# Spreading the token scales of the first stage with TensorE in place of a round trip through DRAM

## The chip, the cores and the metric

The kernel runs on one core of a Trainium2 chip. The metric is the device time of one execution in microseconds (us), as the median over several runs. The core has five engines that work side by side and wait for one another by semaphores: TensorE (PE, matrix products and transposes), VectorE (DVE), ScalarE (ACT), GpSimd (POOL) and SyncE (SP). Here SP issues every DMA transfer, in the order of its own queue.

## The reference

Two layers of a mixer block, one batch of 2048 tokens and 256 context tokens, width 1024. Cut to what matters here:

```python
def rmsnorm(x, g):
    y = xf * lax.rsqrt(jnp.mean(xf * xf, axis=-1, keepdims=True) + NORM_EPS)
    return y * g
...
hx = rmsnorm(x, g_pre) * (1 + scale[:, None]) + shift[:, None]
hc = rmsnorm(ctx, g_pre) * (1 + scale_c) + shift_c
q, k, v, ga, uf, gf, zc, bc, cc, gc = split_cols(hx @ w_in, PROJ_SIZES)
...   # the same columns for hc; rotary on q and k
a = window_attention(q, k, v, kc, vc, sink_b)
f = fourier_mix(uf, w_fourier)
s = short_conv_mix(zc, bc, cc, conv_w, conv_b)
y = gated_merge(a, ga, f, gf, s, gc, w_out)
x_new = x + gate[:, None] * rmsnorm(y, g_post)
```

The step that matters is the first norm of layer 0. Every token has one scale, the rsqrt of its mean square, and the whole row of that token is multiplied by it before the product with `w_in`.

## The kernel before

Tokens are worked on in two halves of 1024 and in chunks of 512 (`CH`); the context is a chunk of 256. A product in float32 is made of three products of split operands: every operand is a high part (`hi`, `wh`) and the rest (`lo`, `wl`), and `proj_k` issues `wh` by `hi`, `wh` by `lo` and `wl` by `hi` (lines 278, 279, 280) for each of 8 blocks `k` of the width. PE contracts over partitions, so tokens must lie along the free dimension, and the width along the 128 partitions.

The first chunk of layer 0 is brought there by PE transposes (line 230, tile `pt`). The later chunks and the context of layer 0 are loaded from a second copy of the input that is transposed already, `xT` and `cT`. There the scale of a token lies along the free dimension, and every partition needs the whole row of scales. The path before is this:

- `pt_r` loads the tokens in the normal layout, one token to a partition, squares them on ACT (`jk`, line 245; `accum_out` gives the sums `ssq`), and takes the rsqrt on POOL (`ru`, `ry`, `rt`, `rr`, lines 96 to 104). The result `rr` has 128 partitions by one column for every 128 tokens. It is stored to a row `rd[slot]` in DRAM (line 248).
- `pt_load` reads the row back onto all 128 partitions (`rb` or `rbc`, line 253) and then loads the transposed input (line 255).
- `pt_post` makes for each `k` the product of input, gain `G` and row (`ht`, DVE, line 266), the high part with the shift added (`big` or `cxh`, ACT, line 267) and the low part (`big` or `cxl`, DVE, line 268).

Slot 3 is the second chunk of half 0, slot 2 the context, slots 0 and 1 the two chunks of half 1, whose scales are worked out at the end of half 0's first products.

`startup` interleaves the modulation vectors, the first chunk and its first four products (`accs`) by a string of letters, `START`; in it `r` calls `pt_r` for slot 3 and the `y`s load and advance `pt_post`. After it come, in `half`, the evacuations of chunk 0 (a SiLU gate `sg`, ACT line 754; rotary of q and k by `qk_chunk`, lines 319 to 324, which use `cosT` and `sinT`), the four products of chunk 1, of the context, and then `form_b`, ten products of 128 tokens each (`accb`, lines 376 to 378) whose outputs leave by `vt` (ACT 382, DVE 383, store to `vs` at 385) and `ut` (ACT 388, store to `us` at 389). `vt` and `ut` have two buffers, the accumulators of tag `acc` four. Then `fft_setup` loads the constants `wf` and `cf` (lines 398 and 400) and multiplies them on PE (`pa`, line 405). `form_b_w` loads and splits the weights of `form_b` (`wbh`, `wbl`). A scheduler orders the instructions of each engine when the kernel is built; at run time every engine goes through its own list in order.

Of the kernel before, what the change touches and what calls it, by code (L numbers as in the profile page):

```python
# [18 lines left out]
NCTX = 256  # L19
# [48 lines left out]
class Kern:  # L68
# [23 lines left out]
    def rsqrt(self, pool, ssq, n, tag, fast=False):  # L92
# [10 lines left out]
        r = pool.tile([128, n], F32, name=f"rr{tag}", tag=f"rr{tag}")  # L103
# [132 lines left out]
    def pt_r(self, slot, base, n, ctx, xt=None):  # L236
# [10 lines left out]
        r = self.rsqrt(self.xp, ssq[:, :nt], nt, "0")  # L247
        nc.sync.dma_start(self.rd[slot, :n].rearrange("(i p) -> p i", p=128), r)

    def pt_load(self, slot, base, n, ctx, rb, tiles):  # L250
        nc = self.nc
        m = KT // len(tiles)
        nc.sync.dma_start(rb, self.rd[slot:slot + 1, :n].broadcast_to([128, n]))
        for i, t in enumerate(tiles):
            nc.sync.dma_start(t, self.I["cT" if ctx else "xT"][:, i * m:(i + 1) * m, base:base + n])
        return [t[:, k] for t in tiles for k in range(m)], rb
# [138 lines left out]
    def fft_setup(self, l, fp, ps):  # L395
        nc = self.nc
        wf = fp.tile([128, 2, 128], F32, name="wf", tag="fbq")
        nc.sync.dma_start(wf, self.I["wf"][l].rearrange("t m d -> m t d"))
        cf = fp.tile([128, 2, 128], F32, name="cf", tag="fd")
        nc.sync.dma_start(cf, self.I["cf"])  # L400
# [218 lines left out]
    def startup(self, ps, hx, blocks, st, wps, gps):  # L619
# [65 lines left out]
        def step(c):  # L685
# [30 lines left out]
            elif c == "r" and "r" not in tail:  # L716
                tail["r"] = 1
                self.pt_r(3, CH, CH, False, self.x1)
            elif c == "y":
                if post1 is None:  # L720
                    step("r")
                    while posts < KT:
                        step("p")
                    tail["h"] = (self.big(), self.big())
                    xT = self.pt_load(3, CH, CH, False, self.x1q.tile([128, CH], F32, name="rb3"),
                                      [t.rearrange("p (k c) -> p k c", c=CH) for t in self.xts()])
                    post1 = self.pt_post(xT, tail["h"], CH, False)
                else:
                    next(post1, None)
# [10 lines left out]
    def half(self, l, half, ps, sv, tail):  # L740
# [4 lines left out]
        with ExitStack() as es:  # L745
# [49 lines left out]
            if first:  # L795
# [6 lines left out]
                with ExitStack() as e0:  # L802
                    gps = self.pool(e0, "gps", bufs=1, side="right")
                    Ws0, accs, p1, hx[1] = self.startup(ps, hx[0], blocks0, st, wps, gps)
# [12 lines left out]
            if not first:  # L817
                if half == 0:
                    hx[1] = self.hx1
                else:  # L820
                    hx[1] = (self.big(), self.big())
                    p1 = self.pt_post(self.x1, hx[1], CH, False) if l == 0 else \
                        self.p0_post(l, ps, "tr", self.x1, hx[1], CH, False)
            chunks = [(hx[c], CH, False, NCTX + base + c * CH,
                       (cosT[:, c * CH:(c + 1) * CH], sinT[:, c * CH:(c + 1) * CH])) for c in range(2)]
            wbs = ExitStack()
            if first:
                xs = [self.x1q.tile([128, D], F32, name=f"xc{i}", tag=f"xq{i}") for i in range(4)]
                self.p0_load(0, 0, NCTX, True, xs[:2])
                self.pt_r(2, 0, NCTX, True, xs)  # L830
                xc = self.pt_load(2, 0, NCTX, True, self.x1q.tile([128, NCTX], F32, name="rbc", tag="xq0"),
                                  [t.rearrange("p (k c) -> p k c", c=NCTX) for t in xs[2:]])
# [5 lines left out]
                pc = self.pt_post(xc, cx, NCTX, True)  # L838
                for k in range(KT):
                    next(p1, None)  # L840
                    for i, (j, ev) in enumerate(blocks0):
                        self.proj_k(accs[i], Ws0[i], h, n, k)
                        if i == 2:
                            next(pc)
                            if k == KT - 1:
                                self.x1pool.close()
                                wb = self.pool(wbs, f"wb{l}{half}", bufs=1)
# [9 lines left out]
            else:  # L857
# [6 lines left out]
                else:  # L864
# [5 lines left out]
                    run(gfs, mid)  # L870
                wb = self.pool(wbs, f"wb{l}{half}", bufs=1)
# [95 lines left out]
            if half == 0:  # L967
                self.x1pool = ExitStack()
                xq = self.pool(self.x1pool, f"xq{l}1", bufs=1, side="right")
                if l == 0:  # L970
                    x0 = self.pt_load(0, HALF, CH, False, st.tile([128, CH], F32, name="rb0", tag="rt", bufs=2),
# [521 lines left out]
```

## Time and profile before

| what | value |
|---|---|
| median of 3 runs | 2089.26 us (2084.22 to 2091.58) |
| span of the profiled execution | 2093.9 us; no other time of this execution is at hand |
| PE busy in it | 1980.6 us, 95% |
| mean granted PE clock | 0.983 |
| DVE, ACT, POOL busy | 59%, 41%, 36% |

The profile is of one execution. A row of a timeline has the start, the duration, the engine, line and operation, and in brackets how long the engine was idle before it and what ended that. A row of waits has the engine and line that waited, what it waited for, the sum, the number of times and the longest. The granted clock is what the chip gave to PE, as a share of full speed. Lines such as L278 are lines of the kernel before; the changed kernel has other numbers for the same code.

### The profile page before, as it was taken

To read this page: it belongs to the slowest core of one execution; us is meant where nothing else is said; L and a number is where in the kernel's file an instruction comes from. 1 tells how busy PE (TensorE), PEld (TensorE's weight loads), DVE (VectorE), ACT (ScalarE), POOL (GpSimd) and SP (SyncE) were. 2 spreads that over 40 slices of the span, in tenths; PEclk is the share of its full clock that TensorE was granted. 3 is DMA by queue.
4 is the path that set the end of the run, shared out by engine and by line. 5 is a ranking of instruction groups with operands and counts; after the bars stand their busy time and mean duration, and the time that the engine had idled before them with its cause. 6 is when DMAs were issued, how large, how long until landed. Compare 5 with 4: busy or idle time off the path is not lost.

```text
span 2093.9 us, 28506 instructions
## 1 busy us (share of the span) xinstructions
PE 1980.6 (95%) x10218; PEld 1671.9 (80%) x10218; DVE 1233.3 (59%) x2218; ACT 855.5 (41%) x1745; POOL 748.0 (36%) x967
## 2 busy tenths in 40 slices
PE   6787999999999899999999999999999989999998
PEld 2686877788788688888887888888887778888886
DVE  7343876445552677777777614333554277777775
ACT  6241211321322556666666412132222266666663
POOL 4221322231432444444444414233243254444443
PEclk9899999999999999999999999999999999999999
DMA  7678666444735744433332625124564654434421
GB/s 303 114 192 223 188 211 219 140 154 137 210 127 163 207 116 122 120 106 106 103 104 106 206 80 130 61 95 122 157 186 136 178 157 113 106 107 111 117 75 41
DMA packets 190333, 295.68 MB, mean 141 GB/s; under 512 B 17624, under 2 KB 121840, under 8 KB 189168
## 3 DMA queue, kind: packets, MB, share of 16 engines
q1 hardware_dynamic: 190192, 293.87, 47.8%
q8 instruction: 80, 1.31, 0.3%
q14 instruction: 61, 0.50, 0.1%
HBM read 218.43 MB, written 75.39 MB: 140 GB/s over the span
## 4 chain that ended last, share of the span: by engine, by line
PE 69%; DMA 10%; DVE 10%; issue 4%; POOL 3%; ACT 2%; SPq 1%; POOLq 0%; DVEq 0%; ACTq 0%
PE acc L280 8%; PE acc L279 8%; PE acc L278 8%; PE tp L1127 6%; PE yp L1176 6%; PE yp L1178 6%; PE yp L1177 6%; PE sp L1081 4%; PE op L1141 3%; PE op L1140 3%; PE sp L1078 3%; PE accb L378 2%; PE accb L376 2%; PE accb L377 2%; DVE jm L161 2%
## 5 line engine op out<-in xcount | busy, mean ns | idle before, releaser
L278 PE MATMUL acc<-big,wh 128*128 128x512 f32 x1152 | 458.9, 399 | 30.6 <-ACT big L267 11.5
L280 PE MATMUL acc<-big,wl 128*128 128x512 f32 x1152 | 454.6, 395 | 4.2 <-POOL wl L90 2.9
L279 PE MATMUL acc<-big,wh 128*128 128x512 f32 x1152 | 455.0, 395 | 0.4 <-POOL big L90 0.4
L90 POOL TENSOR_TENSOR wl<-wr,wh 128x1024 fp32r<-128x1024 f32 x63 | 158.4, 2515 | 400.5 <-ACT wh L84 272.7
L88 DVE TENSOR_TENSOR pl<-tp,ph 128x512 fp32r<-128x512 f32 x320 | 219.2, 687 | 105.6 <-ACT ph L84 102.5
L278 PEld LDWEIGHTS acc<-big,wh 128*128 128x128 f32 x1152 | 219.7, 191 | 75.2 <-ACT big L267 12.0
L1091 ACT ACTIVATE pt<-pt,nm 128x640 f32<-128x640 f32 (+2 forms) x272 | 216.2, 795 | 118.6 <-DVE nm L1088 118.2
L280 PEld LDWEIGHTS acc<-big,wl 128*128 128x128 f32 x1152 | 219.3, 190 | 51.8 <-POOL wl L90 4.0
L279 PEld LDWEIGHTS acc<-big,wh 128*128 128x128 f32 x1152 | 219.7, 191 | 43.7 <-POOL big L90 1.0
L84 ACT ACTIVATE ph<-tp 128x512 fp32r<-128x512 f32 x320 | 188.4, 591 | 132.6 <-PE tp L1127 126.2
L1102 POOL TENSOR_SCALAR pt<-pt,rv 128x640 f32<-128x640 f32 (+2 forms) x272 | 214.2, 808 | 27.2 <-DVE rv L1100 24.2
L1088 DVE CUSTOM_DVE_ANT_0 pt<-sp,mask,nsink 128x640 f32<-128x640 f32 (+2 forms) x256 | 213.4, 841 | 10.1 <-PE sp L1078 5.2
L1127 PE MATMUL tp<-ident,pt 128*128 128x128 f32 x1280 | 196.8, 274 | 12.7 <-POOL pt L1102 12.2
L1127 PEld LDWEIGHTS tp<-ident,pt 128*128 128x128 f32 x1280 | 158.6, 140 | 59.9 <-POOL pt L1102 19.2
L323 POOL TENSOR_TENSOR rs<-rs,sinT 128x512 f32<-128x512 f32 x40 | 68.1, 1703 | 183.6 <-DVE rs L321 154.1
L1081 PE MATMUL sp<-kseg,qt 128*128 128x384 f32 (+1 forms) x512 | 127.5, 330 | 1.1 <-DMA kseg<-ks 1.1
L1176 PE MATMUL yp<-big,hfh 128*128 128x512 f32 x272 | 118.1, 434 | 1.5 <-ACT big L84 1.5
L1078 PE MATMUL sp<-kctx,qt 128*128 128x256 f32 x544 | 114.2, 291 | 3.9 <-DMA qt<-qs 2.1
L1176 PE MATMUL yp<-big,hah 128*128 128x512 f32 x272 | 117.0, 431 | 0.0
L1078 PEld LDWEIGHTS sp<-kctx,qt 128*128 128x128 f32 x544 | 95.3, 189 | 18.4 <-DVE nm L1088 3.3
L1178 PE MATMUL yp<-big,hfl 128*128 128x512 f32 x272 | 107.5, 395 | 0.2
L1177 PE MATMUL yp<-big,hfh 128*128 128x512 f32 x272 | 107.1, 394 | 0.0
(373 smaller groups left out, 3711.5 us busy)
## 6 DMA issues: line engine op xcount, KB each, us to landing
wr<-in_wina SPq DMA_DIRECT2D x76, 512.0 KB, 3.8
qt<-qs SPq DMA_DIRECT2D x34, 512.0 KB, 5.0
wmt<-in_wmodt SPq DMA_DIRECT2D x32, 512.0 KB, 4.2
ftb<-ftd SPq DMA_DIRECT2D x36, 384.0 KB, 3.8
xt<-in_x SPq DMA_DIRECT2D x26, 512.0 KB, 6.4
kseg<-ks SPq DMA_DIRECT2D x24, 512.0 KB, 8.7
xt<-x SPq DMA_DIRECT2D x24, 512.0 KB, 4.5
gat<-gas SPq DMA_DIRECT2D x34, 256.0 KB, 3.2
```

The source lines that it names most:

```text
L88: self.last_v = nc.vector.tensor_tensor(lo, src, f(hi), op=ALU.subtract)
L278: nc.tensor.matmul(a, wh[:, k, :], hi[:, k, :n], start=(k == 0), stop=False)
L279: nc.tensor.matmul(a, wh[:, k, :], lo[:, k, :n], start=False, stop=False)
L280: nc.tensor.matmul(a, wl[:, k, :], hi[:, k, :n], start=False, stop=(k == KT - 1))
L1078: nc.tensor.matmul(sp[:, 256:512], B.q[:, h, :], self.kctx[:, kv, x, :], start=(x == 0), stop=(x == 1))
L1088: nc.vector.tensor_tensor_reduce(d, x, m, scale=-0.125, scalar=self.nsink[:, h:h + 1], op0=ALU.add, op1=ALU.min, accum_out=nm[:, hh:hh + 1])
L1091: nc.scalar.activation(pt, pt, AF.Exp, bias=nm[:, hh:hh + 1], scale=-1.0, accum_out=sm[:, hh:hh + 1])
L1102: nc.gpsimd.tensor_scalar(B.pts[kv][g], B.pts[kv][g], rv[:, g:g + 1], 1.0, op0=ALU.mult, op1=ALU.mult)
L1127: nc.tensor.transpose(tp[:, hh * 128:(hh + 1) * 128], pts[hh][:, t * 128:(t + 1) * 128], self.ident)
L1176: nc.tensor.matmul(yp, hh, wh[:, k, :], start=(i == 0), stop=False)
L1177: nc.tensor.matmul(yp, hh, wl[:, k, :], start=False, stop=False)
L1178: nc.tensor.matmul(yp, hl, wh[:, k, :], start=False, stop=(i == KT - 1))
```

## The change

The scales stay in SBUF (`rk[slot]`). A new `pt_row` spreads them: for each 128 tokens DVE multiplies the identity matrix by zero and adds the token's scale of its partition, which fills a 128 by 128 block `ht` with the scale of each partition along its row; PE transposes it into PSUM (`prb`), where each partition then holds the row; and ACT copies the PSUM tile to `rb`. The row in DRAM, its store and its loads are gone.

Loads are issued elsewhere. Half of chunk 1's `xT` goes to two tiles `xTa` right behind `pt_r`'s own loads, the context in its normal layout ahead of the other half, and `cT` behind that, all within `startup`; `cosT` and `sinT` thus come behind them. `wf` and `cf` are loaded into a pool of their own by `load_wcf`, ahead of `form_b`'s weights, not in `fft_setup`. The same holds for layer 1 and the second halves wherever `fft_setup` runs.

```diff
@@ -89,7 +89,7 @@
         else:
             nc.gpsimd.tensor_tensor(lo, src, f(hi), op=ALU.subtract)
 
-    def rsqrt(self, pool, ssq, n, tag, fast=False):
+    def rsqrt(self, pool, ssq, n, tag, fast=False, r=None):
         g = self.nc.gpsimd
         e = self.nc.vector if fast else g
         u = pool.tile([128, n], F32, name=f"ru{tag}", tag=f"ru{tag}")
@@ -100,7 +100,8 @@
         e.tensor_tensor(t, y, y, op=ALU.mult)
         e.tensor_tensor(t, t, u, op=ALU.mult)
         e.tensor_scalar(t, t, -0.5, 1.5, op0=ALU.mult, op1=ALU.add)
-        r = pool.tile([128, n], F32, name=f"rr{tag}", tag=f"rr{tag}")
+        if r is None:
+            r = pool.tile([128, n], F32, name=f"rr{tag}", tag=f"rr{tag}")
         e.tensor_tensor(r, y, t, op=ALU.mult)
         return r
 
@@ -244,16 +245,25 @@
             jk = self.xp.tile([128, D], BF16, name="jk", tag="jk", bufs=1)
             self.last_sq = nc.scalar.activation(jk, xt[i], AF.Square, bias=0.0, scale=1.0,
                                                 accum_out=ssq[:, i:i + 1])
-        r = self.rsqrt(self.xp, ssq[:, :nt], nt, "0")
-        nc.sync.dma_start(self.rd[slot, :n].rearrange("(i p) -> p i", p=128), r)
-
-    def pt_load(self, slot, base, n, ctx, rb, tiles):
-        nc = self.nc
-        m = KT // len(tiles)
-        nc.sync.dma_start(rb, self.rd[slot:slot + 1, :n].broadcast_to([128, n]))
+        self.rk[slot] = self.cp.tile([128, nt], F32, name=f"rk{slot}")
+        self.rsqrt(self.xp, ssq[:, :nt], nt, "0", r=self.rk[slot])
+
+    def pt_load(self, base, n, ctx, tiles, m, k0=0):
         for i, t in enumerate(tiles):
-            nc.sync.dma_start(t, self.I["cT" if ctx else "xT"][:, i * m:(i + 1) * m, base:base + n])
-        return [t[:, k] for t in tiles for k in range(m)], rb
+            k = k0 + i * m
+            self.nc.sync.dma_start(t, self.I["cT" if ctx else "xT"][:, k:k + m, base:base + n])
+        return [t[:, k] for t in tiles for k in range(m)]
+
+    def pt_row(self, slot, n, ps, rb):
+        nc = self.nc
+        w = self.xp.tile([128, CH], F32, name="ht", tag="ht", bufs=2)
+        pb = ps.tile([128, CH], F32, name="prb", tag="fft")
+        for i in range(n // 128):
+            sl = slice(i * 128, (i + 1) * 128)
+            nc.vector.tensor_scalar(w[:, sl], self.ident, 0.0, self.rk[slot][:, i:i + 1], op0=ALU.mult, op1=ALU.add)
+            nc.tensor.transpose(pb[:, sl], w[:, sl], self.ident)
+        nc.scalar.copy(rb, pb[:, :n])
+        return rb
 
     def pt_post(self, T, h, n, ctx):
         nc = self.nc
@@ -394,10 +404,7 @@
 
     def fft_setup(self, l, fp, ps):
         nc = self.nc
-        wf = fp.tile([128, 2, 128], F32, name="wf", tag="fbq")
-        nc.sync.dma_start(wf, self.I["wf"][l].rearrange("t m d -> m t d"))
-        cf = fp.tile([128, 2, 128], F32, name="cf", tag="fd")
-        nc.sync.dma_start(cf, self.I["cf"])
+        wf, cf = self.wcf
         AB = fp.tile([128, 2, 2, 2, 128], F32R, name="AB")
         pa = ps.tile([128, 2, 2, 128], F32, name="pa", tag="fft")
         for x in range(2):
@@ -716,15 +723,24 @@
             elif c == "r" and "r" not in tail:
                 tail["r"] = 1
                 self.pt_r(3, CH, CH, False, self.x1)
+                t = [gps.tile([128, D], F32, name="xTa", tag=f"wmg{i}") for i in range(2)]
+                tail["T"] = self.pt_load(CH, CH, False, [u.rearrange("p (k c) -> p k c", c=CH) for u in t], 2)
             elif c == "y":
                 if post1 is None:
                     step("r")
                     while posts < KT:
                         step("p")
                     tail["h"] = (self.big(), self.big())
-                    xT = self.pt_load(3, CH, CH, False, self.x1q.tile([128, CH], F32, name="rb3"),
-                                      [t.rearrange("p (k c) -> p k c", c=CH) for t in self.xts()])
-                    post1 = self.pt_post(xT, tail["h"], CH, False)
+                    xs = self.xs = [self.x1q.tile([128, D], F32, name=f"xc{i}", tag=f"xq{i}") for i in range(4)]
+                    self.p0_load(0, 0, NCTX, True, xs[:2])
+                    xT = tail["T"] + self.pt_load(CH, CH, False, [t.rearrange("p (k c) -> p k c", c=CH)
+                                                                  for t in self.xts(2)], 2, 4)
+                    self.xcT = self.pt_load(0, NCTX, True, [t.rearrange("p (k c) -> p k c", c=NCTX) for t in xs[2:]], 4)
+                    tail["T"] = xT
+                    post1 = iter(())
+                elif "T" in tail:
+                    rb = self.pt_row(3, CH, ps, self.x1q.tile([128, CH], F32, name="rb3"))
+                    post1 = self.pt_post((tail.pop("T"), rb), tail["h"], CH, False)
                 else:
                     next(post1, None)
 
@@ -799,9 +815,9 @@
                 xq = self.pool(self.x1pool, "xq0", bufs=1, side="right")
                 self.x1q = xq
                 self.x1 = [xq.tile([128, D], F32, name=f"xq{i}") for i in range(4)]
-                with ExitStack() as e0:
-                    gps = self.pool(e0, "gps", bufs=1, side="right")
-                    Ws0, accs, p1, hx[1] = self.startup(ps, hx[0], blocks0, st, wps, gps)
+                e0 = ExitStack()
+                gps = self.pool(e0, "gps", bufs=1, side="right")
+                Ws0, accs, p1, hx[1] = self.startup(ps, hx[0], blocks0, st, wps, gps)
             else:
                 hx[0] = self.hx0
             cosT = st.tile([128, HALF], F32, name="cosT", tag="cosT")
@@ -821,29 +837,36 @@
                     hx[1] = (self.big(), self.big())
                     p1 = self.pt_post(self.x1, hx[1], CH, False) if l == 0 else \
                         self.p0_post(l, ps, "tr", self.x1, hx[1], CH, False)
+            def load_wcf():
+                if half == 1 or not last_l:
+                    wcp = self.pool(es, f"wcf{l}{half}", bufs=1)
+                    self.wcf = [wcp.tile([128, 2, 128], F32, name=n) for n in ("wf", "cf")]
+                    nc.sync.dma_start(self.wcf[0], self.I["wf"][l].rearrange("t m d -> m t d"))
+                    nc.sync.dma_start(self.wcf[1], self.I["cf"])
+
             chunks = [(hx[c], CH, False, NCTX + base + c * CH,
                        (cosT[:, c * CH:(c + 1) * CH], sinT[:, c * CH:(c + 1) * CH])) for c in range(2)]
             wbs = ExitStack()
             if first:
-                xs = [self.x1q.tile([128, D], F32, name=f"xc{i}", tag=f"xq{i}") for i in range(4)]
-                self.p0_load(0, 0, NCTX, True, xs[:2])
-                self.pt_r(2, 0, NCTX, True, xs)
-                xc = self.pt_load(2, 0, NCTX, True, self.x1q.tile([128, NCTX], F32, name="rbc", tag="xq0"),
-                                  [t.rearrange("p (k c) -> p k c", c=NCTX) for t in xs[2:]])
+                self.pt_r(2, 0, NCTX, True, self.xs)
                 _, n, ctx, tok, rp = chunks[0]
                 for (j, ev), acc in zip(blocks0, accs):
                     ev(acc, n, ctx, tok, rp)
                 h, n, ctx, tok, rp = chunks[1]
                 accs = [ps.tile([128, CH], F32, name="acc", tag="acc") for _ in range(4)]
-                pc = self.pt_post(xc, cx, NCTX, True)
                 for k in range(KT):
                     next(p1, None)
+                    if k == 1:
+                        xc = (self.xcT, self.pt_row(2, NCTX, ps, self.x1q.tile([128, NCTX], F32, name="rbc", tag="xq0")))
+                        pc = self.pt_post(xc, cx, NCTX, True)
                     for i, (j, ev) in enumerate(blocks0):
                         self.proj_k(accs[i], Ws0[i], h, n, k)
-                        if i == 2:
+                        if i == 2 and k:
                             next(pc)
                             if k == KT - 1:
+                                e0.close()
                                 self.x1pool.close()
+                                load_wcf()
                                 wb = self.pool(wbs, f"wb{l}{half}", bufs=1)
                                 WB = self.form_b_w(l, wb)
                         if k == KT - 1:
@@ -868,6 +891,7 @@
                         self.drain(p1)
                         self.x1pool.close()
                     run(gfs, mid)
+                load_wcf()
                 wb = self.pool(wbs, f"wb{l}{half}", bufs=1)
                 fetch(J_K)
                 WB = self.form_b_w(l, wb)
@@ -968,10 +992,11 @@
                 self.x1pool = ExitStack()
                 xq = self.pool(self.x1pool, f"xq{l}1", bufs=1, side="right")
                 if l == 0:
-                    x0 = self.pt_load(0, HALF, CH, False, st.tile([128, CH], F32, name="rb0", tag="rt", bufs=2),
-                                      [t.rearrange("p (k c) -> p k c", c=CH) for t in self.xts()])
-                    self.x1 = self.pt_load(1, HALF + CH, CH, False, xq.tile([128, CH], F32, name="rb1"),
-                                           [xq.tile([128, KT // 2, CH], F32, name=f"xT{i}") for i in range(2)])
+                    x0 = (self.pt_load(HALF, CH, False, [t.rearrange("p (k c) -> p k c", c=CH) for t in self.xts()], 2),
+                          self.pt_row(0, CH, ps, st.tile([128, CH], F32, name="rb0", tag="rt", bufs=2)))
+                    self.x1 = (self.pt_load(HALF + CH, CH, False,
+                                            [xq.tile([128, KT // 2, CH], F32, name=f"xT{i}") for i in range(2)], 4),
+                               self.pt_row(1, CH, ps, xq.tile([128, CH], F32, name="rb1")))
                 else:
                     self.x1 = [xq.tile([128, D], F32, name=f"xq{i}") for i in range(4)]
                     x0 = self.xts()
@@ -1359,7 +1384,7 @@
             self.mask = self.cp.tile([128, 768], F32, name="mask")
             self.G, self.mo, self.mv = {}, {}, {}
             self.ftd = dp.tile([9, 128, 2, 384], F32, name="ftd")
-            self.rd = dp.tile([4, CH], F32, name="rd")
+            self.rk = {}
             self.ggd = dp.tile([DEPTH, 2, D], F32, name="ggd")
             x1 = dp.tile([SEQ, D], F32, name="x1")
             c1 = dp.tile([NCTX, D], F32, name="c1")
```

How it moves the instructions is shown at three places. Names: `rd` is the row in DRAM, `xq` and `xc` are tiles of chunk 1 and of the context, `gs` the stored gate. SP's list before, from the tokens of chunk 1 on:

```order
L196 DMA xq_112<-in_x 128x1024
L196 DMA xq_113<-in_x 128x1024
L809 DMA cosT<-in_cosT 128x1024
L810 DMA sinT<-in_sinT 128x1024
L815 DMA cw_91<-in_convw 128x6
L248 DMA rd<-rr_611 128x4x1
L816 DMA cbias_92<-in_convb 128x2
L196 DMA xc_712<-in_ctx 128x1024
L253 DMA rb_637<-rd 128x512
L255 DMA xt<-in_xT 128x2x512 x4
L196 DMA xc_713<-in_ctx 128x1024
L255 DMA xc_714<-in_cT 128x1024
```

and after:

```order
L254 DMA xTa<-in_xT 128x2x512 x2
L197 DMA xc_639<-in_ctx 128x1024
L197 DMA xc_640<-in_ctx 128x1024
L254 DMA xt<-in_xT 128x2x512 x2
L254 DMA xc_641<-in_cT 128x1024
L254 DMA xc_642<-in_cT 128x1024
L825 DMA cosT<-in_cosT 128x1024
L826 DMA sinT<-in_sinT 128x1024
L831 DMA cw_90<-in_convw 128x6
L832 DMA cbias_91<-in_convb 128x2
L771 DMA gs_81<-sg 128x512 x2
L844 DMA wf<-in_wf 128x2x128
```

The store and the load of the row have gone from between the tokens and `xT`; the rotary tables have moved from ahead of them to behind, and `wf`, with `cf` behind it, stands here. ACT's list before, from the last squares of chunk 1 on:

```order
L245 ACTIVATE jk,ssq<-xq_113 128x1024
L232 ACTIVATE ht<-pt,mo_153,G_154 128x512
L245 ACTIVATE jk,ssq<-xc_712 128x1024
L754 ACTIVATE sg<-acc 128x512 x2
L267 ACTIVATE big<-ht,mo_153 128x512 x2
L319 COPY rt<-acc 128x512 x2
```

and after:

```order
L246 ACTIVATE jk,ssq<-xq_112 128x1024
L233 ACTIVATE ht<-pt,mo_152,G_153 128x512
L246 ACTIVATE jk,ssq<-xc_639 128x1024
L246 ACTIVATE jk,ssq<-xc_640 128x1024
L265 COPY rb_657<-prb 128x512
L770 ACTIVATE sg<-acc 128x512
L277 ACTIVATE big<-ht,mo_152 128x512
```

Both squares of the context now stand ahead of chunk 1's work, and the copy of the row behind them. The four transposes of slot 3 (`prb` for chunk 1) stand in PE's list 15 matmuls behind the last transposes of chunk 0. Those of the context stand among the products of chunk 1; PE's list after there:

```order
L290 MATMUL acc<-big,wl 128x512
L288 MATMUL acc<-big,wh 128x512
L289 MATMUL acc<-big,wh 128x512
L264 MATMUL prb<-ident,ht 128x128
L290 MATMUL acc<-big,wl 128x512
L288 MATMUL acc<-big,wph 128x512
L289 MATMUL acc<-big,wph 128x512
L264 MATMUL prb<-ident,ht 128x128
```

where before there were matmuls alone. The two spreads that they wait for stand in DVE's list between the rotary steps of chunk 0 and the context's `pt_post`:

```order
L88 TENSOR_TENSOR ql<-rt,qh 128x512
L334 TENSOR_TENSOR rt<-rt,rs 128x512
L278 SCALAR_TENSOR_TENSOR big<-ht,mo_152,big 128x512
L263 TENSOR_SCALAR ht<-ident,rk_728 128x128
L88 TENSOR_TENSOR ql<-rt,qh 128x512
L263 TENSOR_SCALAR ht<-ident,rk_728 128x128
L276 SCALAR_TENSOR_TENSOR ht<-xc_641,G_153,rbc 128x256 x2
```

The first of the two has to let a rotary step (`ql`) pass before the second can follow; before, the context's `ht` stood there directly.

More of the change, by code (lines that the diff above doesn't have):

```diff
@@ L246, in pt_r @@
                                                 accum_out=ssq[:, i:i + 1])
-        r = self.rsqrt(self.xp, ssq[:, :nt], nt, "0")
-        nc.sync.dma_start(self.rd[slot, :n].rearrange("(i p) -> p i", p=128), r)
-    def pt_load(self, slot, base, n, ctx, rb, tiles):
-        nc = self.nc
-        m = KT // len(tiles)
-        nc.sync.dma_start(rb, self.rd[slot:slot + 1, :n].broadcast_to([128, n]))
-        for i, t in enumerate(tiles):
-            nc.sync.dma_start(t, self.I["cT" if ctx else "xT"][:, i * m:(i + 1) * m, base:base + n])
-        return [t[:, k] for t in tiles for k in range(m)], rb
+        self.rk[slot] = self.cp.tile([128, nt], F32, name=f"rk{slot}")
+        self.rsqrt(self.xp, ssq[:, :nt], nt, "0", r=self.rk[slot])
+    def pt_load(self, base, n, ctx, tiles, m, k0=0):
+        for i, t in enumerate(tiles):
+            k = k0 + i * m
+            self.nc.sync.dma_start(t, self.I["cT" if ctx else "xT"][:, k:k + m, base:base + n])
+        return [t[:, k] for t in tiles for k in range(m)]
+    def pt_row(self, slot, n, ps, rb):
+        nc = self.nc
+        w = self.xp.tile([128, CH], F32, name="ht", tag="ht", bufs=2)
[6 more added lines that the diff above has]
+        return rb
     def pt_post(self, T, h, n, ctx):
```

## The prediction

> **What bounds the kernel now.** I read the page's head first, then the waits of TensorE (PE) in the stage that the change touches, then the same stage in 5 us windows, then the chain.
>
> ```profile
> span 2093.9 us, 28506 instructions
> PE 1980.6 (95%) x10218; PEld 1671.9 (80%) x10218; DVE 1233.3 (59%) x2218; ACT 855.5 (41%) x1745; POOL 748.0 (36%) x967
> ```
>
> PE is busy 95% of the span, so 113 us are all that removing waits could give. The waits of PE from 40 to 215 us (in total, how often, the longest) say how much of it sits around the change:
>
> ```profile
> PE acc L278 <- ACT big L267: 11.5, 1, 11.5
> PE acc L278 <- ACT ut L388: 6.6, 1, 6.6
> PE acc L278 <- ACT sg L754: 5.7, 1, 5.7
> PE pa L405 <- DMA cf<-in_cf: 5.6, 1, 5.6
> PE accb L376 <- ACT ut L388: 1.1, 1, 1.1
> ```
>
> Five gaps, 30.5 us. What stands around them is seen in the windows (columns: PE, PEld, DVE, ACT, POOL busy; granted clock; DMA share; GB/s):
>
> ```profile
> 65.00:70.00 5.00, 3.69 (x16) 2.65 (x15) 0.00 (x0) 0.00 (x0) 0.00 (x0) 1.00 0.88 31
> 80.00:85.00 5.00, 4.78 (x10) 3.43 (x11) 4.87 (x9) 4.18 (x8) 1.26 (x1) 0.50 1.05 406
> 90.00:95.00 5.00, 5.00 (x24) 4.07 (x23) 5.00 (x7) 1.91 (x3) 0.96 (x1) 1.00 1.01 75
> 160.00:165.00 5.00, 5.00 (x30) 5.00 (x29) 0.29 (x1) 0.51 (x2) 2.40 (x1) 1.00 1.28 24
> 170.00:175.00 5.00, 0.47 (x1) 0.48 (x2) 0.29 (x1) 0.65 (x2) 0.00 (x0) 0.59 0.80 301
> ```
>
> Two things are to be seen. In and after the long gaps the granted clock is 0.50 to 0.59, so a gap costs more than its length. And at 65 and at 160 us the DMA engines are taken while they move 24 to 31 GB/s: something small clogs them. The chain from 54 to 200 us (start, duration) names it:
>
> ```profile
> 56.56 1.16 ACT jk L245 x2
> ...
> 58.08 1.04 POOL ry L98
> ...
> 60.27 10.15 DMA rd<-rr
> 70.86 7.72 DMA xt<-in_xT
> 78.67 0.76 DVE ht L266
> 79.45 0.73 ACT big L267
> ...
> 89.23 5.48 DMA rd<-rr
> ...
> 105.48 0.40 DVE ht L266
> ...
> 134.53 0.45 SPq L248
> 135.03 13.71 DMA xt<-in_x
> ...
> 160.31 13.05 DMA vs<-vt
> ...
> 181.98 2.71 DMA cf<-in_cf
> 184.82 2.05 PE pa L405 x8
> ```
>
> The store of the scale row (512 numbers of 4 bytes, each a piece of its own in DRAM, L248) takes 10.15 us; the row's load and those of xT stand behind it in SP's queue, so chunk 1 starts late. A third such store is issued at 134.53, and the fourth stands in SP's queue a little ahead of the vs store of 160.31; the transfers issued next to them take 13.71 and 13.05.
>
> **The change, gap by gap.** What a gap costs with its slow tail, from PE's timeline (start, duration, idle before):
>
> ```profile
> 80.22 0.79 PE L278 MATMUL acc<-big,wh 128*128 128x512 f32 x1 [11.53 <-ACT big L267]
> 85.74 0.40 PE L278 MATMUL acc<-big,wh 128*128 128x512 f32 x1
> 85.97 0.39 PE L279 MATMUL acc<-big,wh 128*128 128x512 f32 x1
> ...
> 111.00 0.58 PE L278 MATMUL acc<-cxh,wh 128*128 128x256 f32 x1 [5.72 <-ACT sg L754]
> 116.43 0.28 PE L280 MATMUL acc<-cxh,wl 128*128 128x256 f32 x1
> ...
> 174.53 0.79 PE L278 MATMUL acc<-big,wh 128*128 128x512 f32 x1 [6.58 <-ACT ut L388]
> 177.94 0.39 PE L280 MATMUL acc<-big,wl 128*128 128x512 f32 x1
> ...
> 186.52 0.77 PE L279 MATMUL acc<-big,wh 128*128 128x512 f32 x1
> 188.20 0.39 PE L280 MATMUL acc<-big,wl 128*128 128x512 f32 x1
> ```
>
> Gap 1, the row of chunk 1. From 80.22 to 85.74 stand 12 matmuls, at 0.46 where full clock gives 0.23 (85.74 to 85.97): 5.52 - 12 x 0.23 = 2.8 lost. With the 11.53 of idling 14.3. What replaces the bounce: POOL has the scales just before 60.27, as now. Four multiplications of the identity on VectorE (DVE), 128 x 128; four PE transposes; one ScalarE (ACT) copy of 128 x 512. The rows next of kin:
>
> ```profile
> 60.44 0.60 PE L230 MATMUL pt<-ident,xt 128*128 128x128 f32 x4
> 61.95 0.43 DVE L82 CAST big<-ht 128x512 fp32r<-128x512 f32 x1 [5.28 <-ACT ht L232]
> 80.75 1.05 ACT L319 COPY rt<-acc 128x512 f32<-128x512 f32 x2
> ```
>
> DVE is idle for 5.28 us before 61.95, and four products cost at most 4 x 0.40 (a 128 x 256 one at 105.48), so the spread is free and ends near 61.9. The transposes come 15 matmuls (3.5 us) after the pt transposes of 60.44, so near 64.3; they take up to 0.6 of PE. PE idles 11.53 up to 80.22, so chunk 0 ends at 68.7, and near 69.3 now. The copy stands on ACT behind the last ht (to 61.9, since the cast waits for it) and the two squares of the context, 1.16 each (64.2), needs the transposes (64.9) and takes 0.53: 65.4. Then ht 0.76, big 0.73 and lo as long as ht give 67.7: chunk 1 is ready 1.6 us ahead of PE. The first two xT loads go out ahead of the context's, which wait only for the squares of chunk 1's first tiles, done before the 56.56 ones; both are out some 3 us or more before that, near 50 and 53 (counted by hand), and have 8 us or more to land; the second two near 61.5, first used at k = 4, eleven us after the start (12 matmuls of 0.23 a k, 2.75). So gap 1 goes whole. Its cover is those 1.6 us, and the loads of the context, which must land before their squares; nothing is stored word by word then. If they land at 66, PE waits 2 to 3.
>
> Gap 2, the context. Its bounce (89.23) goes, and cT is loaded near 62, in front of all of chunk 1. From 111.00 to 116.43 stand 25 starts (two unrecorded) at 0.21; at 0.115 they would take 2.9: 2.5 lost, 8.2 with the gap. New: two spreads, which the DVE queue holds behind the rotary work of chunk 0, and two PE transposes in PE's own queue among the matmuls of k = 1 of chunk 1 and after. PE comes to the second near 81.5; DVE, which is full in the window at 90 (5.00 of 5.00), is there between 81 and 84 when its rows of before are counted from the new start. So PE waits 0 to 3; I take 2, nearer the upper end since DVE has no idle time there. Behind it stand a copy and, for eight k, ht and lo at 0.40 and an ACT step between: some 7.4 us, done near 93, when PE has chunk 1 behind it. That tie may leave 0 to 1.
>
> Gap 3, 1.1 us: an accb of form_b waits for an ACT copy that is behind squares, and these behind the 13.71 of xt. Gap 4: 6.58 plus 177.94 - 174.53 - 8 x 0.23 = 1.6, is 8.2: the last ut waits for vt, vt for the buffer that the 13.05 store holds. Both go if the word stores do, since transfers then take what their like take (KB each, median to landing):
>
> ```profile
> xt<-in_x SPq DMA_DIRECT2D x26, 512.0 KB, 6.4
> ```
>
> Bounds: nothing, if the other loads and not the words slow these; 9.3 if all goes. I take all: 24 GB/s at a full share is what words look like, and the 301 GB/s at 170 us, after them, is what the loads look like.
>
> The Trainium skill ("DMA: Bandwidth & Descriptors", Specifications) puts the least transfer for full rate at 512 B; below it the engine reads, modifies and writes. By that rule the words clog, and the window at 160 us agrees. By the same page's fixed 2 us for a transfer alone ("Anatomy of one DMA") a bounce would cost some 4 us, and an estimate from that would leave gaps 3 and 4 unexplained; the 10.15 decides against it.
>
> Gap 5, 5.55: PE waits for cf, issued at 181.98. Now wf and cf are issued behind the cT and gs rows, near 68 us, with 80 us to land. With the slow tail (188.20 - 186.52 - 4 x 0.23 = 0.8) and eight pa products at half clock (2.05, against 1.2 by the four of 60.44) it is 7.2.
>
> Moved past in SP's queue: cosT and sinT, which were loaded ahead of the scale row, go behind xT and cT now, near 64; the 3 MB from 61 on take 7 to 10 us at the 301 to 406 GB/s of the windows: landed by 72. Their first user on DVE stood here:
>
> ```profile
> 87.18 0.68 DVE L322 TENSOR_TENSOR rt<-rt,cosT 128x512 f32<-128x512 f32 x1
> ```
>
> that is 7.0 us after the start of chunk 1, near 76 then: covered by 4 us.
>
> For the second half: eight spreads in the DVE queue among ql and vt, eight transposes on PE after form_b (two times 0.6, 1.2) and two ACT copies beside PE's work. The four spreads of the last slot stand before the fourth vt and wait for that slot's last square; form_b's accb wait in gap 3 came four accumulators after the late one, so there is some 12 us of cover. Price 0 to 3, taken 0.
>
> **Sum.** 14.3 + 8.2 + 1.1 + 8.2 + 7.2 = 39.0 saved; 0.6 + 0.3 + 1.2 for transposes and 2.0 of waiting are 4.1 added: 34.9. The profiled execution spans 2093.9, 4.6 above the median of the runs (2089.3) and 2.3 above the highest. That gives 2059.0 in the profile and 2054.4 by the median; I say 2054. From 190 us on nothing that bounds PE is touched, so what is won stays.
>
> The clock after a short gap:
>
> ```profile
> 150.94 0.44 PE L376 MATMUL accb<-wbh,big 128*128 128x384 f32 x1 [1.11 <-ACT ut L388]
> ```
>
> The next matmul takes 0.44, not the 0.58 to 0.79 of the long gaps, so I price the 2 us at the context without a slow tail; with gap 1's, 2.8, they would be 4.8. The Trainium skill ("TensorE: Matmul & The Clock Gate", Part 1) halves the clock only after an idle window of about 3.4 us; by that, too, 2 us cost no more than 2.
>
> **Rivals.** (A) Part of it: the head of chunk 1 closes, later gaps stay or return. For: gaps 3 and 4 rest on the reading that the words slow the stores, not the loads beside them, and a block of loads moves earlier, where it may collide (406 GB/s at 80). Against: 24 GB/s. Without gaps 3 and 4 the gain is 25.6, 2064; with gap 1 alone 14.3 less 0.6 + 1.2, 2077. (B) No change: what chunk 1 waits for is its xT loads, held by buffers, and the row was hidden behind them. Against: xT is issued at 70.86, after the bounce, in the chain. It would give 2083 to 2095. (C) Slower: a scale that is late holds DVE at the last slot's spread; vt backs up and form_b runs out of accumulators. It decides from 12 us of cover plus the 35 gained plus 6, an xt load of over 50 us; the longest in the chain is 13.7. Near 2100.
>
> **How the numbers follow.** Full gain, 30 to 40 us (2049 to 2059, with the runs' scatter 2046 to 2062): 0.66. A: 0.24, most of it between 2062 and 2077. B: 0.06. C: 0.04. The range 2046 to 2077 holds nearly all of the first and most of A. A change under 0.3%, 6.3 us, is about what runs of this kernel can't tell from none. Faster 0.91, same 0.05, slower 0.04.
>
> **What would show it.** In the profile after: no rd; PE without the 11.5 us wait, chunk 1 starting near 69; granted clock 1.00 in the windows from 70 to 100; the context's matmuls near 93, with at most a short wait at prb; form_b done near 146; no long vs or xt there; pa without a wait for cf near 150, and PE 36 us earlier at the matmul that is now at 188.20. The forecast is wrong if prb waits for DVE for over 5 us, if rb is late because ACT waits for the context's loads, or if the ut copy still stops PE near 146.

## The result, and the profile after

The kernel after takes 2050.98 us (median of 4 runs, 2048.78 to 2054.88), the kernel before 2090.42 in the same comparison (4 runs, 2084.22 to 2091.98). The ratio is 0.982, with a 95% interval of 0.980 to 0.984, so the change saves 39.4 us. 2054 was forecast. The profiled execution of after took 2048.78 in all and spans 2046.7.

```profile
span 2046.7 us, 28533 instructions
PE 1972.0 (96%) x10232; PEld 1668.4 (82%) x10232; DVE 1241.5 (61%) x2232; ACT 858.9 (42%) x1749; POOL 746.3 (36%) x967
```

Before, five waits of PE from 40 to 215 us summed to 30.5 us. After, the longest waits in that stage are these:

```profile
PE prb L264 <- DVE ht L263: 2.0, 1, 2.0
PE pmr L666 <- DVE wql L88: 1.2, 2, 0.8
```

All five are gone. The two short ones at pmr were there before, too. One wait is new: PE waits for the spread of the context's scales, 2.0 us. The windows that answer to those shown of before (same columns):

```profile
65.00:70.00 5.00, 5.00 (x24) 4.11 (x22) 4.66 (x8) 4.18 (x8) 1.41 (x3) 1.00 0.99 356
80.00:85.00 5.00, 3.01 (x15) 2.17 (x14) 4.09 (x9) 3.11 (x6) 0.00 (x0) 1.00 0.65 145
90.00:95.00 5.00, 5.00 (x34) 4.53 (x33) 4.97 (x9) 4.77 (x10) 2.00 (x1) 1.00 0.66 238
135.00:140.00 5.00, 5.00 (x31) 5.00 (x30) 0.58 (x2) 1.30 (x4) 0.00 (x0) 1.00 1.04 394
```

The clock is 1.00 in all of them, and a full DMA share moves 356 to 394 GB/s at 65 and 135 us, where before it moved 31 and 24 in the windows that answer to them (65 and 160 us). PE's rows at the marks of the prediction:

```profile
63.85 0.60 PE L264 MATMUL prb<-ident,ht 128*128 128x128 f32 x4
68.41 0.39 PE L288 MATMUL acc<-big,wh 128*128 128x512 f32 x1
...
82.58 0.30 PE L264 MATMUL prb<-ident,ht 128*128 128x128 f32 x1 [1.99 <-DVE ht L263]
82.95 0.40 PE L288 MATMUL acc<-big,wph 128*128 128x512 f32 x1
...
92.64 0.28 PE L288 MATMUL acc<-cxh,wh 128*128 128x256 f32 x1
...
146.01 0.33 PE L388 MATMUL accb<-wbh,cxl 128*128 128x384 f32 x1
146.18 1.05 PE L412 MATMUL pa<-wf,cf 128*128 128x128 f32 x8
```

Set against the same instructions before, these give how far PE is ahead at each mark. The forecast is that of the prediction's last part and of its sum.

| mark | before | after | ahead | forecast |
|---|---|---|---|---|
| first matmul of chunk 1 | 80.22 | 68.41 | 11.8 | 10.9 |
| first of the context | 111.00 | 92.64 | 18.4 | 18 |
| last of form_b | 167.60 | 146.01 | 21.6 | 21.6 |
| 18th matmul of the next products | 188.20 | 150.95 | 37.3 | 36 |
| span | 2093.9 | 2046.7 | 47.2 | 34.9 |

Up to the fourth mark it came as worked out. The 10 us behind that were not forecast, and they are taken up below.

### The profile page after: what moved, and what is told of

It reads as the page before. It is cut to its first block, busy times and chain, and to the rows that moved or that the text cites. A ratio compares the mean times of both kernels' runs of the same rounds, so it can differ in the third digit from the quotient of the medians.

```text
span 2046.7 us, 28533 instructions
## 1 busy us (share of the span) xinstructions
PE 1972.0 (96%) x10232; PEld 1668.4 (82%) x10232; DVE 1241.5 (61%) x2232; ACT 858.9 (42%) x1749; POOL 746.3 (36%) x967
## 4 chain that ended last, share of the span: by engine, by line
PE 70%; DVE 11%; DMA 10%; POOL 3%; issue 3%; ACT 2%; SPq 1%; DVEq 0%; POOLq 0%; ACTq 0%
PE acc L290 8%; PE acc L288 8%; PE acc L289 8%; PE tp L1152 7%; PE yp L1201 6%; PE yp L1203 6%; PE yp L1202 6%; PE sp L1106 4%; PE op L1166 3%; PE op L1165 3%; PE sp L1103 3%; PE accb L386 2%; PE accb L388 2%; PE accb L387 2%; DVE jm L162 2%
```

## Experiments

All ratios are to the kernel before, run beside it.

**A second profile of both kernels.** Nothing is edited.

> The kernel before, once more, for a second profile. Theory (the five gaps come from the order of the work): 11.5, 5.7, 1.1, 6.6 and 5.6 us again, each within 1 us, and a span nearer to the median, 2086 to 2090, with the difference to the first profile behind 200 us. Rival (the clogged transfers vary): the gaps differ by more than 3 us in sum.

> The kernel after, once more, for a second profile. Theory: one wait of about 2 us at prb in the stage, span 2047 to 2052, the lead over the second profile of before at pa within 1 us of that of the first pair (37.5). Rival: other waits in the stage, a lead off by more than 3 us.

Before spans 2081.7 this time, below what was expected, and the waits of PE in the stage are these:

```profile
PE acc L278 <- ACT big L267: 10.3, 1, 10.3
PE acc L278 <- ACT sg L754: 5.5, 1, 5.5
PE pa L405 <- DMA cf<-in_cf: 5.2, 1, 5.2
PE acc L278 <- ACT ut L388: 5.1, 1, 5.1
```

They sum to 26.1, not 30.5, so the rival was right there: four gaps are the same in kind and place but each is 0.2 to 1.5 us shorter, and gap 3 is missing. After spans 2050.4. Its wait at prb is 2.08, and this time it has a slow tail:

```profile
83.04 0.30 PE L264 MATMUL prb<-ident,ht 128*128 128x128 f32 x1 [2.08 <-DVE ht L263]
83.75 0.63 PE L289 MATMUL acc<-big,wph 128*128 128x512 f32 x1
```

In the second pair after is ahead by 30.7 at the mark behind pa and by 31.3 at the end, so the lead that was expected there, 37.5 within 1, was missed. The first pair gave 37.3 and 47.2. The mean of the two at the end, 39.3, is what the medians give; at the mark it is 34.0. Each pair lies some 8 us from that mean at the end, so one pair of profiles is good to no more than that.

**Constants early, alone.** The kernel before, with `load_wcf` of the change.

```diff
-        wf = fp.tile([128, 2, 128], F32, name="wf", tag="fbq")
-        nc.sync.dma_start(wf, self.I["wf"][l].rearrange("t m d -> m t d"))
...
+        wf, cf = self.wcf
...
+                                load_wcf()
```

> The kernel before with one part of the change, the Fourier constants wf and cf loaded ahead of form_b's weights. Theory (each gap has its own cause): PE's 5.6 us wait at pa is gone with its slow tail, the 6.6 us wait for the ut copy stays; 7 us faster than before, 2083 (2079 to 2087). Rival (the gaps share a cause, so that the work only waits elsewhere): pa no longer waits, but the end of the stage comes less than 3 us earlier, 2088 to 2091.

Measured: 2085.46 against 2087.57, ratio 0.999 (0.998 to 1.000). PE does not wait at pa, but its waits of the stage now hold

```profile
PE cpf L393 <- DVE cuh L82: 13.0, 1, 13.0
PE acc L278 <- ACT big L267: 10.2, 1, 10.2
PE acc L278 <- ACT sg L751: 7.5, 1, 7.5
PE accb L376 <- ACT ut L388: 4.2, 1, 4.2
```

The rival held in its main point: the wait went to the next product, which needs what the us stores wrote. Gap 5 is no cause of its own in the kernel before. The 2 us hide two parts. Matched matmul by matmul with the first profile of before (with the second in brackets), PE is 3.6 us (7.7) behind at the end of this stage and wins 6.6 (4.2) back further on. Where it wins them is seen in the run "Constants late in after" below.

**Fewer pieces in two of the four stores.** The kernel before; slots 0 and 1 (second half) are stored 16 bytes a piece.

```diff
-        nc.sync.dma_start(self.rd[slot, :n].rearrange("(i p) -> p i", p=128), r)
+        nc.sync.dma_start(self.rd[slot, :n].rearrange("(p i) -> p i" if slot < 2 else "(i p) -> p i", p=128), r)
```

> The kernel before, but the scales of slots 0 and 1 are stored as 128 pieces of 16 bytes, not 512 of 4; the row is then in another order, so tokens of the second half get each other's scales (the amount of work is the same). Theory (the number of small pieces clogs the DMA engines): the xt load and the vs store issued next to these stores take under 7 us each, where they took 13.7 and 13.1, and PE's waits for the ut copies (1.1 and 6.6) shrink to 0 and under 2; some 8 us faster, 2082 (2079 to 2086). Rival (the 2 MB of loads slow them): both stay over 10 us, waits unchanged, 2090.

Measured: 2071.51, ratio 0.993 (0.991 to 0.995). That ratio and the medians (2087.57 beside it) give 15 to 16 us, twice what was expected. DMA issues from 120 to 180 us (KB each, median us to landing), first of the kernel before:

```profile
xt<-in_x SPq DMA_DIRECT2D x4, 512.0 KB, 11.7
vs<-vt SPq DMA_DIRECT2D x9, 128.0 KB, 8.8
rd<-rr SPq DMA_DIRECT2D x2, 2.0 KB, 11.7
```

and with 16-byte pieces:

```profile
xt<-in_x SPq DMA_DIRECT2D x4, 512.0 KB, 5.1
vs<-vt SPq DMA_DIRECT2D x10, 128.0 KB, 4.7
rd<-rr SPq DMA_DIRECT2D x2, 2.0 KB, 3.5
```

The bytes are the same, and so are the loads beside them; only the pieces differ, in number and in size. (The two medians of rd hide a spread: 13.4 and 9.9 us with words, 5.5 and 1.4 with 16-byte pieces.) The waits for ut are gone from PE's list, and at pa 0.2 us is left of the wait for cf.

So gaps 3, 4 and 5 share one cause, the two word stores. In the kernel before, the chain behind the vs store of 13.05 us goes on through the last vt and ut and an xT load to the issue of wf (L398), with cf behind it:

```profile
174.51 0.38 SPq L389
...
175.42 6.06 DMA xt<-in_xT
181.54 0.38 SPq L398
```

Together with the run before this, it shows that wf and cf need no other place for gap 5 to close.

Is it the number of the words? The kernel before has a store of half as many, the 256 scales of the context (1.0 KB). Here are the first store of 512 words and this one (KB, us from issue to landing):

```profile
rd<-rr SPq DMA_DIRECT2D x1, 2.0 KB, 10.2
rd<-rr SPq DMA_DIRECT2D x1, 1.0 KB, 9.9
```

Half the words took as long, so the number alone does not set the time; the runs with larger pieces change number and size together and do not separate the two. The packets beside the first store, from 61 to 63.2 us and from there to its landing at 70.4, show where its time does not go:

```profile
DMA packets 688, 0.07 MB, mean 31 GB/s; under 512 B 672, under 2 KB 672, under 8 KB 688
DMA packets 41, 0.17 MB, mean 23 GB/s; under 512 B 0, under 2 KB 0, under 8 KB 41
```

All the small pieces stand in the first 3 us behind the issue. In the 7 us after them only large ones are recorded, at 23 GB/s; what these and the store wait for is not in the trace.

**The same for all four slots.** The kernel before; the tokens that are only squared are loaded four to a partition (`src[base:base + n].rearrange("(p i) d -> i p d", p=128)`), so that the 16-byte pieces stand in token order.

> The kernel before, with the tokens that are only squared loaded four (two for the context) to a partition, so that the scales are stored as 128 pieces of 16 (8) bytes in token order; row loads, order and everything else as before. Theory (the count of pieces sets the store's time and the clog): store 3 to 5 us in place of 10, PE's wait ahead of chunk 1 falls from 11.5 to 5 to 7, gaps 3 to 5 are gone as with slots 0 and 1 alone; 2064 (2059 to 2069). Rival (a round trip costs its latency whatever the pieces): the wait ahead of chunk 1 stays over 9.5 us, 2071.

Measured: 2062.21, ratio 0.987 (0.984 to 0.989). SP's rows (start, time to issue) and PE's wait ahead of chunk 1:

```profile
60.57 0.33 SPq L253 DMA_DIRECT2D rd<-rr  x1
...
61.99 0.34 SPq L258 DMA_DIRECT2D rb<-rd  x1
62.42 4.59 SPq L260 DMA_DIRECT2D xt<-in_xT  x4
```

```profile
PE acc L283 <- ACT big L272: 4.0, 1, 4.0
```

The row's load, which waits for the store, goes out 1.4 us after it, where it was 10.2. Some 26 of the 39 us are thus to be had without TensorE, by storing 128 pieces in place of 512. The other 11 to 13 are not the spread's alone, since this kernel also has the loads and the constants in their old places. Matched matmul by matmul, PE is 7.6 us behind after at the mark behind pa, 8.1 at 195 us and 13.7 at 234; the run with late constants below has that last step, too. So the spread and the places of the loads together are worth some 8 us here. The 4.0 us that are left ahead of chunk 1 end with a load of xT, which stands behind the row's load in SP's queue.

**The bounce of slot 3 back.** The kernel after, with the row of chunk 1 through DRAM.

```diff
+        if slot == 3:
+            nc.sync.dma_start(self.rd[slot, :n].rearrange("(i p) -> p i", p=128), self.rk[slot])
...
+            nc.sync.dma_start(rb, self.rd[slot:slot + 1, :n].broadcast_to([128, n]))
+            return rb
```

> The kernel after, with the scale row of chunk 1 alone taken through DRAM again (store of 512 words, load onto all partitions); the loads stay where the change put them. Theory (the bounce itself is on the path): the store takes about 10 us from 60, the row's load 4 to 6 more, chunk 1 starts at 76 to 79, a PE wait of 7.5 to 10 us plus a slow tail of 2.8; 2062 (2058 to 2067). Rival (the order of the loads is what the change gains by): chunk 1 starts by 71, 2051 to 2053.

Measured: 2068.93, ratio 0.991 (0.989 to 0.993), 18 us above after and beyond the expected range. PE waits, and SP's rows:

```profile
82.17 0.80 PE L293 MATMUL acc<-big,wh 128*128 128x512 f32 x1 [13.72 <-ACT big L282]
```

```profile
60.26 0.37 SPq L251 DMA_DIRECT2D rd<-rk  x1
62.26 9.68 SPq L256 DMA_DIRECT2D xc<-in_cT  x2
72.03 0.66 SPq L262 DMA_DIRECT2D rb<-rd  x1
```

The bounce is on the path, with the loads already in place. It is dearer than before: the two cT loads stood in the issue for 9.7 us beside the words (0.89 in after), and the row's load behind them went out 1.6 us later than before and took 8.4 us to land (6.6 before).

**The old places of the loads.** The kernel after, with xT, context, cT, cosT and sinT loaded where before had them.

```diff
-                t = [gps.tile([128, D], F32, name="xTa", tag=f"wmg{i}") for i in range(2)]
-                tail["T"] = self.pt_load(CH, CH, False, [u.rearrange("p (k c) -> p k c", c=CH) for u in t], 2)
...
+                    xT = self.pt_load(CH, CH, False, [t.rearrange("p (k c) -> p k c", c=CH) for t in self.xts()], 2)
```

> The kernel after, with the scale rows spread by PE, but xT, the context and cT loaded where the kernel before had them (no xTa tiles). Theory (the bounce was the cause of gap 1): xT goes out near 61 and its first piece lands 4 to 9 us later, chunk 1 starts between 69 and 72; the context's squares come later, so its scale row and its matmuls wait some 2 to 6 us more; 2055 (2051 to 2060). Rival (the earlier loads give most of the gain): chunk 1 starts after 75, 2061 or more.

Measured: 2052.01, ratio 0.984 (0.982 to 0.985). That cannot be told from after. No wait stands ahead of chunk 1, so the moved loads give at most a microsecond or two. The wait at prb was 2.45 here, and six matmuls behind it ran at half clock:

```profile
82.55 0.45 PE L264 MATMUL prb<-ident,ht 128*128 128x128 f32 x1 [2.45 <-DVE ht L263]
82.65 0.77 PE L290 MATMUL acc<-big,wpl 128*128 128x512 f32 x1
```

**Two word stores added to after.** Slots 0 and 1 are stored again, and nothing reads them.

```diff
+        if slot < 2:
+            nc.sync.dma_start(self.rd[slot, :n].rearrange("(i p) -> p i", p=128), self.rk[slot])
```

> The kernel after, which also stores the scales of slots 0 and 1 to DRAM as 512 words of 4 bytes each, as the kernel before did; nothing reads them. Theory (these two stores, through SP's queue, made gaps 3, 4 and 5): xt beside the first and vs beside the second take over 10 us, the chain of squares behind them is late, and most of the 15 us that the 16-byte pieces gave comes back; PE waits for a ut copy, and the time is 2059 to 2067. Rival (in the new order form_b has slack enough, or the loads were to blame): the transfers are long but PE waits under 2 us in the stage, 2051 to 2054.

Measured: 2063.12, ratio 0.988 (0.985 to 0.990), 12 us above after. The xt load beside the first store takes 12.97 us (chain), and the wait that grows is

```profile
PE cpf L405 <- DVE cuh L82: 10.0, 1, 10.0
```

The cost was as expected, its place for the most part was not: PE waits 1.8 and 1.3 us for ut copies, and 10.0 where the us stores are read back.

**Constants late in after.**

```diff
-                                load_wcf()
...
+        nc.sync.dma_start(wf, self.I["wf"][l].rearrange("t m d -> m t d"))
```

> The kernel after, with wf and cf loaded in fft_setup as before. Theory (they came late only because SP's queue was held by the vs store ahead of them): issued near 146, landed near 149, PE waits 0 to 3 us at pa; 2052 (2050 to 2054). Rival (gap 5 has its own cause, the place of these loads): PE waits 5 us and more with a slow tail, 2056 to 2059.

Measured: 2062.01, ratio 0.987 (0.985 to 0.989), 11 us above after. Neither theory has that. In the stage the theory held, with 0.7 us of waiting at pa:

```profile
150.83 1.16 PE L415 MATMUL pa<-wf,cf 128*128 128x128 f32 x8 [0.66 <-DMA cf<-in_cf]
```

PE is 2.5 behind after at 195 us, and then 5.2 at 234 and 12.5 at 350. The largest step is at 343, where before, too, has a wait of 2.66 (at 375.90); after has 0.35 there:

```profile
343.34 0.79 PE L290 MATMUL acc<-big,wl 128*128 128x512 f32 x1 [2.66 <-POOL wl L90]
```

```profile
319.93 0.50 PE L290 MATMUL acc<-big,wl 128*128 128x512 f32 x1 [0.35 <-POOL wl L90]
```

The scheduler has put DVE's list in another order there. With late constants (and in before) it reads

```order
L88 TENSOR_TENSOR th<-tr,th 128x384
L358 SCALAR_TENSOR_TENSOR cy<-cTm,cw_90,cy 128x1023
L977 TENSOR_TENSOR cTc<-acc,czc 128x256
L82 CAST wh<-wr 128x1024
```

and in after

```order
L358 SCALAR_TENSOR_TENSOR cy<-cTm,cw_90,cy 128x1023
L82 CAST wh<-wr 128x1024
L976 TENSOR_TENSOR cTc<-acc,czc 128x256
```

The weights' cast `wh`, which POOL and then PE wait for, stands behind a step `th` of the Fourier table there and ahead of `cTc` here. So the constants' place changed an order 190 us later. All profiles of this document bear it out: the five with late constants (before twice, before_rows01, perm_all, wcf_late) have the first order, the eight with early ones the second, wcf_only among them. The waits for `wl` from 215 us to some 400 sum to 2.9 to 4.7 us in the five and to 0.5 to 1.7 in the eight; before and wcf_only read

```profile
PE acc L280 <- POOL wl L90: 2.9, 2, 2.7
PE acc L280 <- POOL wl L90: 1.5, 1, 1.5
```

Matched matmul by matmul with after, the step at 231 us (2.7 here) also stands in the five, with 2.1 to 4.6 us, and in none of the eight. So both steps go with the place of the constants in the kernel before and in the one after, and there wcf_only won back what it had lost in the stage. That this order makes the wait is still read from the profiles and was not tried alone; which instruction makes the step at 231 us, and what comes behind 350, stays open.

**The context's spread on POOL, and in a tile of its own.**

```diff
-            nc.vector.tensor_scalar(w[:, sl], self.ident, ...)
+            (nc.gpsimd if slot == 2 else nc.vector).tensor_scalar(w[:, sl], self.ident, ...)
```

> The kernel after, with the context's two spreads on POOL, right behind the rsqrt steps there, not on DVE. Theory (the wait at prb is DVE's queue): PE's 2.0 us wait at prb is gone, the context's matmuls follow chunk 1 without a new wait; 2049 (2046 to 2051). Rival (the wait moves to the context's own chain): PE waits 1 to 2 us at the context's first matmul or elsewhere in the stage, 2051.

Measured: 2054.63, ratio 0.984 (0.981 to 0.987). Nothing is gained. PE waits longer at prb, and POOL's row says why:

```profile
79.67 3.41 POOL L263 TENSOR_SCALAR ht<-ident,rk 128x128 f32<-128x128 f32 x2 [3.99 <-DVE big L278]
82.77 0.85 PE L264 MATMUL prb<-ident,ht 128*128 128x128 f32 x2 [3.62 <-POOL ht L263]
```

POOL waited for a low part of chunk 1: the spread shares the two ht buffers with chunk 1. And it then took 3.41 us for the two spreads, which DVE does in 0.28 each (after, 82.15 and 82.95). So the next kernel gives the spread a tile of its own, on DVE:

```diff
-        w = self.xp.tile([128, CH], F32, name="ht", tag="ht", bufs=2)
+        w = self.x1q.tile([128, n], F32, name="hw") if slot == 2 else self.xp.tile([128, CH], F32, name="ht", tag="ht", bufs=2)
```

> The kernel after, with a tile of its own for the context's spread, where it had taken turns with the ht tiles of chunk 1. Theory (the spread waited for an ht tile to come free, in DVE's order behind the rotary work): its rows now stand right behind the first ht of chunk 1, the wait of 2.0 us at prb is gone or under 0.5, and the context's matmuls start some 2 us earlier; 2049 (2046 to 2052). Rival (the scales of the context are late themselves, and now hold up chunk 1): PE waits over 1 us in chunk 1, 2051 or more.

Measured: 2049.07, ratio 0.981 (0.978 to 0.984), against 0.982 for after. The wait at prb is gone, and one of 1.0 us at the context's accumulators takes its place:

```profile
92.06 0.39 PE L288 MATMUL acc<-cxh,wh 128*128 128x256 f32 x1 [0.99 <-ACT sg L770]
```

The context starts at 92.06 and not 92.64. By the runs the two kernels can't be told apart.

## Why the prediction was right, point by point

- **Gap 1** went whole, as its step had it: bounce3 brings it back with the loads in place, loads_before leaves it shut with the loads in their old places. Of the steps in it, transposes at 64.3 (63.85), copy by 65.4 and chunk 1 with no wait all stood.
- **Gap 2.** The wait at prb of 0 to 3, taken as 2, was 1.99 and 2.08, and the context started at 92.64, forecast near 93. The named cause, DVE's queue, was not the whole: own_tile leaves the spread on DVE, gives it a tile of its own, and the wait is gone, so the shared ht buffers held it. The step "priced without a slow tail" holds for one profile and not for the other, where PE lost some 1.7 us more.
- **Gaps 3 and 4** went, and the words did it: the same bytes and the same loads with a quarter of the pieces, each four times as large, close them (before_rows01), and the words bring 12 us back (words01). The choice of "all" between nothing and 9.3 was right.
- **Gap 5** is the step that failed in its reason, though not in its size. The prediction gave it 7.2 us for the new place of wf and cf. Alone that place saves 2 us or nothing (wcf_only), and without it the gap is 0.7 (wcf_late). The words on SP's queue had made it; 16-byte pieces close gaps 3 to 5 for 15 us, and the forecast's 1.1 + 8.2 + 7.2 is 16.5. That its size came out is luck: the change removed the words as well.
- **"From 190 us on nothing that bounds PE is touched"** was wrong. The place of the constants is worth 11 us in after, nearly all of it further on. The prediction looked for instructions that move in the first stage and not for what the scheduler does with the same change later: the `th` step ahead of the weights' cast at 343 us, and the step at 231.
- **The sum.** 34.9 was forecast and 39.4 came by the medians. At the mark behind pa, where the change was to have done all, the two pairs give 34.0 in the mean against 36; the rest, some 5 us, came later and was not forecast. The gaps were taken from an execution whose span lies 12 us above that of the second profile, so they may be some us too large for the median (30.7 ahead at the mark in the second pair); what the constants gave further on stands against that. So the median came out within 3 us in part by two errors that offset each other, which is luck. The transposes priced at 2.1 cost about half of it: the matmul behind the first four starts 0.35 us after them (64.20), the one behind the eight 0.79 (347.82).
- **Rivals.** (A), (B) and (C) didn't happen. (A)'s reading, that the loads and not the words slow the stores, is ruled out by before_rows01. Its other half, a block of loads that collides, is not seen: the windows with 356 to 394 GB/s are ones in which PE is full.

The Trainium skill ("DMA: Bandwidth & Descriptors", Specifications) speaks of pieces under 512 B as slow. The runs agree for 4 bytes, but pieces of 16 bytes are under that too, and their store was done in 1.4 us where the words took 10.2, so that size is not the bound that tells here. The 2 us that the prediction takes from that page of the Trainium skill stand in a section on transfers that GpSimd issues; here SP issues them all.

## What to carry to other kernels

A small store can cost far more than its bytes when it is cut into words: look for a full DMA share at a few GB/s in the windows, and count what else stands in that queue. When several waits follow one another in a stage, try the suspected cause alone before giving each its own price: three gaps here had one cause, and to close the last of them alone moved it. Where a scheduler orders the instructions, compare the lists far behind the change as well, and don't read less than some 8 us from a single pair of profiles.

## What the runs showed of the hardware that was not expected

- A store of 2 KB in 512 words took 9.1 to 13.4 us from issue to landing (before, before_again, wcf_only, bounce3, words01), one of 1 KB in 256 words 9.2 to 9.9 (before, before_again, wcf_only), and one of 2 KB in 128 pieces of 16 bytes 1.4 to 5.6 (before_rows01, perm_all). Neither the bytes nor the number of pieces alone gives these times.
- Word stores hold up SP's issue too: two cT loads took 9.68 us to issue beside one, 0.89 without it.
- PE's clock after a short idle time: 1.11 (before) and 1.99 us (after) left no tail, 2.08 (after_again) and 2.45 (loads_before) were followed by six to eight matmuls at half speed. The Trainium skill ("TensorE: Matmul & The Clock Gate", Part 1) has an idle window of about 3.4 us as the bound; here shorter ones were enough, and the measurement decides. Their length alone does not tell: 1.98 us in perm_all (316.92) brought half speed, and so did 2.66 in wcf_late (343.34), while the same 2.66 in before_rows01 did not:

```profile
359.44 0.50 PE L280 MATMUL acc<-big,wl 128*128 128x512 f32 x1 [2.66 <-POOL wl L90]
359.77 0.40 PE L278 MATMUL acc<-big,wh 128*128 128x512 f32 x1
```
